# Retention queries projected feature-major, with a sine table kept in SBUF, in a hybrid decoder trunk

## The chip, the cores and the metric

The kernel runs on one core of one Trainium2 chip. The metric is the device time of one execution in microseconds; the time given for a kernel is the median of several executions. A core has five engines with instruction queues of their own: TensorE (PE in the profile; its weight loads are shown apart as PEld), VectorE (DVE), ScalarE (ACT), GpSimd (POOL) and SyncE (SP), which here only issues DMAs. PSUM has eight banks, into which TensorE writes.

## The reference

Two layers (`DEPTH`), sequence 1024, width 1024, batch 1, all in float32. Per layer:

```python
shift, scale, gate = jnp.split(c_act @ w_mod + b_mod, 3, axis=-1)
h = rms_norm(x, pre_gain) * (1.0 + scale) + shift
proj = h @ w_in        # columns: attention (q, k, v, gate), retention (q, k, v, gate), GLA
...
rq, rk = apply_rotary(rq, positions, ret_freq), apply_rotary(rk, positions, ret_freq)
r = retention(rq, rk, rv)
r_out = rms_norm(r) * silu(rg)
...
y = concat([a_out, r_out, g_out]) @ w_out
x = x + gate * rms_norm(y, post_gain)
```

`apply_rotary` splits a head's 64 features into halves x1, x2 and returns x1 cos - x2 sin and x2 cos + x1 sin, with an angle per position and frequency. Attention and retention have different frequencies, 32 each. `retention` has four heads of 64 features and works in chunks of 128 positions. Position i of a chunk has the decay g^(i+1) on its query and g^(-(i+1)) on its key (g is a constant of the head); the masked product of queries and keys is multiplied with the values, a 64x64 state per head carries what lies before the chunk, and after each chunk the state is multiplied by g^128. The result is RMS-normalised per position and head, with no gain.

## The kernel before

**Matmuls.** Every projection is a product of two float32 numbers split into a high and a low part (`F32R` tiles, index 0 and 1): three passes `(0,0), (1,0), (0,1)` over eight slices of the contraction, 24 matmuls per result (`accum`). `project` makes a token-major result: the normalised input `hT` of one tile of 128 positions is the loaded operand and 256 columns of a weight stream. `project_T` makes a feature-major result: 128 weight columns are loaded and 512 positions stream; the attention queries and gates use it. Weights arrive as 256 KB stages (`st`, from SyncE's queue), are split by ScalarE, VectorE and GpSimd, and lie in places of two arenas.

**Stages of a layer.** The gates of GLA and retention (gg, rg) by pairs of tiles; then retention, for each of four pairs `p` the projections rq, rk, rv of both tiles; then GLA, the attention keys and values, the attention queries and gates, and the output projection. In the first layer, before the gates, the first modulation is computed and x is normalised, modulated and transposed (`pre`, L657).

**Retention.** For rq and rk each, `ret_rot` (L1157) rotates a 128x256 result out of PSUM with five VectorE operations (`rotary`, L818) against `sincos`, the token-major table in SBUF, and multiplies it by the decay of the query (`qdec`) or the key (`kdec`, which holds the factor 1/8 too). rv is copied by ScalarE. `ret_core` (L1163) transposes q and k of a tile, two transposes each, copies all four blocks out of PSUM at once, multiplies scores, masks them by VectorE, and multiplies by v and by the state `stR`. `head_norm_gate` squares, reduces and normalises with `rstd_of` (L635), whose `eps` is an immediate.

**Tables.** `tables` (L414) computes all angles, 128 positions by 8 tiles by 64 frequencies, reduces them and takes sines and cosines: some fifteen VectorE operations of 512 elements in four `t2` tiles, with a pause between each two. `tables_T` (L447) then makes, for each pair, a copy of the attention half repeated for four heads, four transposes, a ScalarE copy with the factor 1/8, and a store to `tabS` in DRAM. `attn_rot` (L862) reads it back for the attention queries.

**Modulation.** The later modulations read `w_mod` in slices of 256 KB into tiles of their own (`mod_stage`, tag `sm8`, `BMOD` = 5 of them) and accumulate on VectorE (L367), a slice per step.

**Order.** TensorE's instructions run in the order in which the program writes them. A planner sets this order: `clk` adds the modelled time of each matmul, every other piece of work is a generator in `jobs` that yields a delay (a value of the table `L`, `key@1` for layer 1) or a flag, and `pump` runs whatever is due, after every seven matmuls. `await_flag` moves `clk` forward where something is not due. Thus the delays in `L` decide after how many matmuls a transpose or a small product is put into TensorE's stream; TensorE stands if its input is not there by then. The other engines' orders and SyncE's are set by the compiler's scheduler from the program's order and the dependences. `table_job` (L1460) starts with the layer; retention starts after `await_flag("tables")` (L1504).

**Buffers** that the change touches: `mm`, three PSUM banks for projections, and `aux`, five for all else; `kT0` and `kT1`, one buffer each, which hold two tiles of x at the start, the attention keys' high and low parts, and (kT1) the GLA gate input `gaT`; `mx`, two large tiles.

Of the kernel before, what the change touches and what calls it, by code (L numbers as in the profile page):

```python
# [60 lines left out]
def host_constants():  # L61
# [12 lines left out]
    c["qdec"] = (gam[None, :] ** (i[:, None] + 1.0)).astype(f)  # L74
    c["kdec"] = (0.125 * gam[None, :] ** (-(i[:, None] + 1.0))).astype(f)
# [18 lines left out]
def trunk(ctx: ExitStack, tc: tile.TileContext, ins, cst, out):  # L94
# [17 lines left out]

    def t2(dt=F32):
        return gp.tile([P, 512], dt, tag="t2", name=nm("t2"), bufs=B2)
# [6 lines left out]

    def mod_stage():
        return gp.tile([P, 512], F32, tag="sm8", name=nm("ms"), bufs=BMOD)
# [142 lines left out]
    tabS = dr.tile([NP_, P, 2, 256], F32, name="tabS")  # L266
# [147 lines left out]
    def tables():  # L414
        PIF = float(np.nextafter(np.float32(math.pi), np.float32(0)))
        ang = t2()
        V.tensor_tensor(ang.rearrange("p (t k) -> p t k", t=NT), posf.unsqueeze(2).to_broadcast((P, NT, 64)),
                        freq.unsqueeze(1).to_broadcast((P, NT, 64)), ALU.mult)
        yield
        nn = t2()  # L420
# [7 lines left out]
        n2 = t2()  # L428
# [4 lines left out]
        red = t2()  # L433
# [13 lines left out]
    def tables_T():  # L447

        for p in range(NP_):
            yield L["tt1"]  # L450
            rep_ = t2()
            V.tensor_copy(rep_.rearrange("p (s t h k) -> p s t h k", s=2, t=2, h=4),
                          sincos[:, 2 * p:2 * p + 2, :, 0:32].rearrange("p t s k -> p s t k").unsqueeze(3)
                          .to_broadcast((P, 2, 2, 4, 32)))
            yield L["tt2"]
            pt = aux()
            for i in range(4):
                transp(pt[:, i * P:(i + 1) * P], rep_[:, i * P:(i + 1) * P], ident)
            tb = t2()
            A.activation(tb, pt, AF.Copy, scale=0.125)  # L460
            nc.sync.dma_start(tabS[p], tb.rearrange("p (s n) -> p s n", s=2))
# [172 lines left out]

    def rstd_of(ss, w, scale, eps):  # L635
        r = small(w)
        V.tensor_scalar(r, ss, scale, eps, ALU.mult, ALU.add)  # L637
# [133 lines left out]
    qdec = cload("qdec")  # L771
    kdec = cload("kdec")
# [89 lines left out]
    def attn_rot(l, hf, g, w_):  # L862
# [3 lines left out]
        for s, d in ((0, sn), (1, cs)):  # L866
            nc.sync.dma_start(d.rearrange("p (s n) -> p s n", s=2),
                              tabS[2 * hf:2 * hf + 2, :, s, :].rearrange("s p n -> p s n"))
# [288 lines left out]
    def ret_rot(t, src, dec_):  # L1157
        r = t1()
        rotary(r, src, 4, t, 1)
        eng("rdec").tensor_tensor(h4(r), h4(r), dec_.unsqueeze(2).to_broadcast((P, 4, 64)), ALU.mult)  # L1160
# [564 lines left out]
```

## Time and profile before

| | |
|---|---|
| Median of 3 runs | 993.5 us (992.89 to 995.62) |
| Profiled execution | 992.12 us |
| its span, first to last instruction | 990.4 us |
| Mean granted TensorE clock | 0.991 |
| Instructions | 19626 |

The page gives for each engine its busy time, its share of the span and its instructions. A group line has: line, engine, operation, output<-inputs by tile names, shapes, count; then busy time and the mean of one in ns; then the idle time before it with what ended it. A wait line has: the waiting engine, tile and line, what it waited for, then microseconds in total, times, and the longest. A line of the timeline has: start, length, engine, line, what, count. A line of DMA issues has: what, queue, operation, count, KB each, median us from issue to landing.

### The profile page before, as it was taken

How to read it: one execution, taken by the hardware profiler on the slowest of the kernel's cores; microseconds unless marked ns; L12 is line 12 of the kernel's file. 1: busy time of each engine (PE TensorE's matmuls, PEld its weight loads, DVE VectorE, ACT ScalarE, POOL GpSimd, SP SyncE). 2: the span in 40 equal slices, each digit the busy share in tenths (PEclk: the TensorE clock that was granted, in tenths of full speed). 3: DMA queues.
4: the chain of work that ended last, by engine and by line, in shares of the span. 5: the costliest groups of instructions: out<-in, count | busy, mean ns of one | idle time of the engine just before them, and what ended most of it. 6: DMA issues, size and time to landing. Idle time of an engine off the chain costs nothing. (4 is left out here: it accounts for less than half of the span.)

```text
span 990.4 us, 19626 instructions
## 1 busy us (share of the span) xinstructions
PE 964.5 (97%) x7133; PEld 824.7 (83%) x7133; DVE 683.3 (69%) x1679; ACT 409.5 (41%) x1152; POOL 244.7 (25%) x310
## 2 busy tenths in 40 slices
PE   5899999999999999999999999999999999999996
PEld 1599999888998777778889999998999877777775
DVE  3879858687766777654787266775765577676975
ACT  2577312333332656623555242133332257664331
POOL 2322011233310224420124100122322034544000
PEclk8899999999999999999999999999999999999999
DMA  8853414532234355587565121342132433388783
GB/s 319 297 187 96 153 49 137 162 123 79 67 122 146 91 177 160 166 269 240 200 223 179 61 87 33 97 146 68 50 97 86 128 89 121 111 267 269 256 267 132
DMA packets 112305, 148.77 MB, mean 150 GB/s; under 512 B 12064, under 2 KB 63820, under 8 KB 112208
## 3 DMA queue, kind: packets, MB, share of 16 engines
q1 hardware_dynamic: 100176, 132.19, 42.4%
q10 hardware_dynamic: 12032, 15.33, 4.4%
q8 instruction: 56, 0.92, 0.4%
q14 instruction: 41, 0.34, 0.1%
HBM read 109.20 MB, written 36.18 MB: 147 GB/s over the span
## 5 line engine op out<-in xcount | busy, mean ns | idle before, releaser
L168 PE MATMUL mm<-arena 128*128 128x256 f32 (+2 forms) x1824 | 300.8, 319 | 1.7 <-ACT arena L707 1.5
L168 PE MATMUL mm<-arena,arena 128*128 128x256 f32 (+2 forms) x1824 | 296.0, 316 | 0.0
L168 PEld LDWEIGHTS mm<-arena 128*128 128x128 f32 x1824 | 255.3, 191 | 26.1 <-issue 3.6
L168 PEld LDWEIGHTS mm<-arena,arena 128*128 128x128 f32 x1824 | 251.6, 188 | 24.4 <-issue 4.0
L638 POOL TENSOR_TENSOR sm<-sm,mhalf 128x1 f32<-128x1 f32 (+1 forms) x64 | 55.7, 870 | 329.0 <-DVE sm L637 293.6
L168 PE MATMUL mm<-arena,mx 128*128 128x512 f32 (+1 forms) x564 | 130.9, 387 | 0.5 <-DMA mx<-mixS 0.3
L168 PEld LDWEIGHTS mm<-arena,mx 128*128 128x128 f32 x564 | 101.4, 188 | 24.7 <-issue 1.5
L152 ACT ACTIVATE t<-aux 128x256 f32<-128x256 f32 (+2 forms) x124 | 55.7, 466 | 65.1 <-PE aux L183 44.1
L152 ACT ACTIVATE arena<-st 128x512 fp32r<-128x512 f32 x94 | 56.1, 628 | 49.7 <-PE mm L168 21.2
L932 POOL TENSOR_TENSOR smx<-smx,sm 128x512 f32<-128x512 f32 x32 | 35.1, 1097 | 130.2 <-DVE sm L931 109.4
L536 DVE TENSOR_TENSOR arena<-st,arena 128x512 fp32r<-128x512 f32 x77 | 61.6, 821 | 2.9 <-ACT arena L152 1.6
L536 POOL TENSOR_TENSOR arena<-st,arena 128x512 fp32r<-128x512 f32 x31 | 44.3, 1431 | 75.5 <-ACT arena L152 68.0
L928 ACT ACTIVATE smx<-smx,sm 128x129 f32<-128x129 f32 x128 | 49.9, 392 | 29.9 <-DVE sm L925 29.9
L183 PE MATMUL aux<-c_ident,t 128*128 128x128 f32 (+1 forms) x292 | 47.9, 283 | 6.3 <-DVE t L669 5.7
L367 DVE SCALAR_TENSOR_TENSOR acc<-ms,c_act,acc 128x512 f32<-128x512 f32 x60 | 45.6, 759 | 5.3 <-DMA ms<-in_w_mod_dram 4.4
L183 PEld LDWEIGHTS aux<-c_ident,t 128*128 128x128 f32 (+1 forms) x292 | 35.4, 145 | 12.6 <-DVE t L669 7.3
L976 ACT ACTIVATE t<-aux 128x256 f32<-128x256 f32 x32 | 12.3, 384 | 76.6 <-PE aux L168 69.2
L168 PEld LDWEIGHTS aux<-t,mx 32*128 32x128 f32 (+1 forms) x896 | 40.0, 187 | 4.0 <-issue 2.4
L701 ACT ACTIVATE t<-aux,mod,mod 128x128 f32<-128x128 f32 x68 | 26.0, 460 | 39.4 <-PE aux L183 21.6
L168 PE MATMUL aux<-t,mx 32*128 32x32 f32 (+1 forms) x896 | 41.3, 272 | 0.2 <-DVE modg L381 0.2
L1251 DVE SCALAR_TENSOR_TENSOR t<-t,sm,t 128x512 f32<-128x512 f32 x32 | 24.0, 781 | 22.4 <-DMA t<-in_x_dram 16.7
L923 DVE COPY_PREDICATED smx<-c_curmask,aux 128x256 f32<-128x256 int32 x64 | 25.4, 446 | 16.6 <-ACT smx L152 13.2
(224 smaller groups left out, 1382.5 us busy)
## 6 DMA issues: line engine op xcount, KB each, us to landing
st<-in_w_in_dram SPq DMA_DIRECT2D x96, 256.0 KB, 4.1
ms<-in_w_mod_dram SPq DMA_DIRECT2D x64, 256.0 KB, 4.1
mx<-mixS SPq DMA_DIRECT2D x20, 512.0 KB, 5.4
st<-in_w_last_dram SPq DMA_DIRECT2D x36, 256.0 KB, 3.6
wm<-in_w_mod_dram SPq DMA_DIRECT2D x12, 512.0 KB, 6.6
t<-in_x_dram SPq DMA_DIRECT2D x24, 256.0 KB, 5.5
mixS<-t SPq DMA_DIRECT2D x40, 128.0 KB, 2.4
mixS<-t ACTq DMA_DIRECT2D x32, 128.0 KB, 1.9
```

Source lines behind the costliest of these rows:

```text
L152: A.activation(dst, src, AF.Copy)
L168: T.matmul(dst, lhsT, rhs, start=start, stop=stop)
L183: T.transpose(dst, src, idn)
L367: V.scalar_tensor_tensor(acc, wt, c_act[:, k:k + 1], acc, ALU.mult, ALU.add)
L536: e.tensor_tensor(lo, st, f(hi), ALU.subtract)
L638: G.tensor_tensor(r, r, mhalf[:, :w], ALU.pow)
L701: A.activation(hf[:, ks], at[kt], AF.Identity, scale=gain, bias=shift)
L923: V.copy_predicated(sv, curmask.unsqueeze(1).to_broadcast((P, 2, P)), pv[:, :, n // P - 1, :])
L928: A.activation(sm[:, h, :], sm[:, h, :], AF.Exp, bias=mx[:, h:h + 1], accum_out=sums[:, h:h + 1])
L932: eng("pn").tensor_tensor(sm[:, :, 0:128], sm[:, :, 0:128], rs.unsqueeze(2).to_broadcast((P, 4, P)), ALU.mult)
L976: A.activation(sq, po, AF.Square)
L1251: V.scalar_tensor_tensor(xt[j], yg[j], r, xt[j], ALU.mult, ALU.add)
```

## The change

- The queries of retention come from a new `ret_q`, once per pair of tiles and feature-major: `project_P` loads 128 weight columns and streams 256 positions, twice. The rotation's sine products are four VectorE operations on 32 partitions each, which write to the neighbouring block of 32 partitions, then one product with the cosines and one sum, all of 512 elements per partition. The table for it, `tab` (features by positions, sine and cosine, with the factor 1/8), stays in SBUF.
- The result lies in `kT0` (pairs 0 and 1) and `kT1` (pairs 2 and 3). `ret_core` no longer transposes q; it transposes k alone and waits for the flag of the queries, then takes its slice.
- Neither q nor k is multiplied by a decay. The key's decay is put on v (`vdec`), by VectorE in place of ScalarE's copy; the query's decay is a factor of a whole row, which the normalisation takes out, with a constant per row and head (`reps`) in place of `4 * EPS`.
- The tables are computed in one `mx` tile instead of four `t2` tiles, behind the last modulation so far. Two blocks of four transposes make both halves (attention and retention); they are stored to `tabS`, from which four DMAs of 256 KB fill `tab`; sixteen stores of 64 KB write the attention half to `tabA`, repeated for four heads. Retention waits for `tab` in the planner.
- `BMOD` goes from 5 to 3.
- Nearly all delays in `L` have other values, with new ones for `tt3`, `tt4`, `tt6` and `rq1`. Among them: `tb1` 24.5 to 12.59, `tb2` 0.75 to 0.89, `tt1` 8.6 to 7.12, `tt2` 5.32 to 1.62, `mod2` 4.0 to 3.86, `ld2` 0.21 to 1.2.

```diff
-    c["qdec"] = (gam[None, :] ** (i[:, None] + 1.0)).astype(f)
-    c["kdec"] = (0.125 * gam[None, :] ** (-(i[:, None] + 1.0))).astype(f)
+    c["reps"] = (4.0 * EPS * gam[None, :] ** (-2.0 * (i[:, None] + 1.0))).astype(f)
+    c["vdec"] = (gam[None, :] ** (-(i[:, None] + 1.0))).astype(f)
...
-    tabS = dr.tile([NP_, P, 2, 256], F32, name="tabS")
+    tabS = dr.tile([2, 2, 32, S], F32, name="tabS")
+    tabA = dr.tile([4, 32, 2, S], F32, name="tabA")
+    tab = cp.tile([P, 2, S], F32, name="tab")
...
-        ang = t2()
-        V.tensor_tensor(ang.rearrange("p (t k) -> p t k", t=NT), posf.unsqueeze(2).to_broadcast((P, NT, 64)),
-                        freq.unsqueeze(1).to_broadcast((P, NT, 64)), ALU.mult)
+        tmp = mix_tile(F32).rearrange("p a k q -> p (a k q)").rearrange("p (i n) -> p i n", i=4)
+        ang, nn, n2, red = (tmp[:, i] for i in range(4))
+        with tc.issue_after(mark[3].ins):
+            V.tensor_tensor(ang.rearrange("p (t k) -> p t k", t=NT), posf.unsqueeze(2).to_broadcast((P, NT, 64)),
+                            freq.unsqueeze(1).to_broadcast((P, NT, 64)), ALU.mult)
...
-        for p in range(NP_):
-            yield L["tt1"]
-            rep_ = t2()
-            V.tensor_copy(rep_.rearrange("p (s t h k) -> p s t h k", s=2, t=2, h=4),
-                          sincos[:, 2 * p:2 * p + 2, :, 0:32].rearrange("p t s k -> p s t k").unsqueeze(3)
-                          .to_broadcast((P, 2, 2, 4, 32)))
-            yield L["tt2"]
+        tbs = []
+        for i in range(2):
+            yield L["tt1"] if i == 0 else L["tt2"]
             pt = aux()
-            for i in range(4):
-                transp(pt[:, i * P:(i + 1) * P], rep_[:, i * P:(i + 1) * P], ident)
+            for t in range(4):
+                transp(pt[:, t * P:(t + 1) * P], sincos[:, 4 * i + t].rearrange("p s k -> p (s k)"), ident)
             tb = t2()
             A.activation(tb, pt, AF.Copy, scale=0.125)
-            nc.sync.dma_start(tabS[p], tb.rearrange("p (s n) -> p s n", s=2))
+            ts = slice(512 * i, 512 * i + 512)
+            nc.sync.dma_start(tabS[:, :, :, ts].rearrange("s c k n -> (s c k) n"), tb)
+            tbs.append(tb)
+        yield L["tt3"]
+        for b in range(4):
+            nc.sync.dma_start(tab[32 * b:32 * b + 32], tabS[:, 1].rearrange("s k n -> k s n"))
+        flag("tab", L["tt6"])
+        for i in range(2):
+            for h in range(4):
+                yield L["tt4"]
+                for j in range(2):
+                    nc.sync.dma_start(tabA[h, :, j, 512 * i:512 * i + 512], tbs[i][64 * j:64 * j + 32])
...
+    def project_P(pm, l, p, w, c):
+        h = hT[(l, p)]
+        accum(pm, lambda a, k: w[:, a, k, c:c + P], lambda b, k: h[:, b, k, 0:256])
...
-    def ret_rot(t, src, dec_):
+    def ret_q(l, p, w):
+        pm = mm()
+        for c in range(2):
+            project_P(pm[:, 256 * c:256 * c + 256], l, p, w, c * P)
...
+        sn, cs = (tab[:, i, 256 * p:256 * p + 256].unsqueeze(1).to_broadcast((P, 2, 256)) for i in range(2))
+        u, x = t2(), t2()
+        for b in range(4):
+            r = slice(32 * b, 32 * b + 32)
+            o = two(x)[32 * (b ^ 1):32 * (b ^ 1) + 32]
+            if b % 2:
+                V.scalar_tensor_tensor(o, two(pm)[r], -1.0, sn[r], ALU.mult, ALU.mult)
+            else:
+                V.tensor_tensor(o, two(pm)[r], sn[r], ALU.mult)
+        V.tensor_tensor(two(u), two(pm), cs, ALU.mult)
+        if p % 2 == 0:
+            rqT[0] = gp.tile([P, NT * P], F32, tag=f"kT{p // 2}", name=nm("rq"), bufs=1)
+        q = rqT[0][:, 512 * (p % 2):512 * (p % 2) + 512]
+        V.tensor_tensor(q, u, x, ALU.add)
+        flag(("rq", l, p), L["rq1"])
+        return two(q)
...
-            transp(pt[:, j * P:(j + 1) * P], q[:, j * P:(j + 1) * P], ident)
-            transp(pt[:, (2 + j) * P:(3 + j) * P], k[:, j * P:(j + 1) * P], ident)
-        tt_ = t2()
-        qT = tt_[:, 0:256]
-        kTt = tt_[:, 256:512]
-        copy("rT", tt_, pt)
+            transp(pt[:, j * P:(j + 1) * P], k[:, j * P:(j + 1) * P], ident)
+        kTt = t1()
+        with tc.high_priority():
+            copy("rT", kTt, pt[:, 0:256])
+        yield (0.0, ("rq", l, t // 2))
+        qT = q[:, :, P * (t % 2):P * (t % 2) + P]
...
-        await_flag("tables")
+        await_flag("tab")
         for p in range(NP_):
             last = p == NP_ - 1
-            rr = {}
-            for name in ("rq", "rk", "rv"):
+            q = ret_q(l, p, used(l, "rq"))
+            pump()
...
-                        copy("rv", v, src)
-                        job(ret_core(l, t, rr[("rq", tt)], rr[("rk", tt)], v))
+                        V.tensor_tensor(h4(v), h4(src), vdec.unsqueeze(2).to_broadcast((P, 4, 64)), ALU.mult)
+                        job(ret_core(l, t, q, ks[tt], v))
...
-B2, B1, BS, BST, MMB, SMB, BMOD = 10, 8, 11, 5, 3, 3, 5
+B2, B1, BS, BST, MMB, SMB, BMOD = 10, 8, 11, 5, 3, 3, 3
```

47 lines of the change are left out of this document (27 added, 20 removed).

## The prediction

> **What bounds the kernel now.** I read the page's busy shares first, then stretches of time, then TensorE's waits, then the timeline inside the retention stage.
>
> ```profile
> PE 964.5 (97%) x7133; PEld 824.7 (83%) x7133; DVE 683.3 (69%) x1679; ACT 409.5 (41%) x1152; POOL 244.7 (25%) x310
> ```
>
> Columns of the stretches: from:to, length, then busy time (and instructions) of PE, weight load, DVE, ACT, POOL, granted clock, DMA share, GB/s.
>
> ```profile
> 46.00:980.00 934.00, 930.58 (x7000) 806.19 (x6998) 652.21 (x1607) 390.80 (x1105) 230.57 (x287) 1.00 0.45 142
> ...
> 50.00:75.00 25.00, 25.00 (x211) 24.95 (x210) 19.99 (x55) 19.89 (x60) 6.79 (x15) 1.00 0.60 188
> 75.00:100.00 25.00, 24.84 (x206) 24.57 (x205) 24.82 (x55) 17.36 (x39) 5.77 (x10) 1.00 0.32 99
> 100.00:125.00 25.00, 25.00 (x218) 24.41 (x217) 20.84 (x64) 8.24 (x16) 1.86 (x1) 1.00 0.45 146
> ...
> 600.00:625.00 25.00, 25.00 (x217) 24.47 (x216) 15.43 (x52) 5.94 (x11) 2.02 (x2) 1.00 0.11 33
> ```
>
> From 46 to 980 us TensorE is idle for 934.00 - 930.58 = 3.4 us at the full clock. So the length of its own instruction stream sets the end: an instruction taken out of it is worth its whole pitch, and delays set better can win back at most 3.4 us there. The waits say the same:
>
> ```profile
> PE aux L183 <- DVE posr L408: 5.8, 1, 5.8
> PE aux L183 <- DVE t L669: 5.7, 3, 4.0
> PE mm L168 <- ACT arena L707: 1.5, 1, 1.5
> ```
>
> These three, 13.0 us, lie in the start or touch it, before layer 0's table work; nothing in the diff removes them.
>
> **Terms on TensorE.** The group that loses instructions, as the page has it, and the ends that its mean hides (matmuls are pipelined, so 283 ns is a latency):
>
> ```profile
> L183 PE MATMUL aux<-c_ident,t 128*128 128x128 f32 (+1 forms) x292 | 47.9, 283 | 6.3 <-DVE t L669 5.7
> ```
>
> In layer 1's retention stage, blocks of 2 and of 6 transposes, each with the instruction that follows:
>
> ```profile
> 606.66 0.38 PE L183 MATMUL aux<-c_ident,t 128*128 128x128 f32 x2
> 606.80 0.60 PE L168 MATMUL mm<-arena,arena 128*128 128x256 f32 x3
> ...
> 636.29 0.82 PE L183 MATMUL aux<-c_ident,t 128*128 128x128 f32 x6
> 636.86 3.08 PE L168 MATMUL mm<-arena,arena 128*128 128x256 f32 x24
> ```
>
> ```profile
> 101.73 0.60 PE L183 MATMUL aux<-c_ident,t 128*128 128x128 f32 x4
> 102.08 1.08 PE L168 MATMUL mm<-arena 128*128 128x256 f32 x7
> ```
>
> The next matmul starts 0.14, 0.57 and 0.35 us after the block's start, so a transpose more in a block costs (0.57 - 0.14)/4 = 0.107 us; the bare average of the shortest is 0.07. The change removes the two transposes of q in each `ret_core`: 2 x 8 tiles x 2 layers = 32, or 3.4 us. The tables need two blocks of four instead of four: -2 x 0.35 = -0.7 us. Together -4.1 us, with ends 40 x 0.07 = 2.8 and 40 x 0.107 = 4.3.
>
> The projection of q keeps its amount: 24 matmuls of 256 columns per tile before, 24 per half of the columns and pair of tiles after, so 48 per pair either way. What is loaded and what streams change places; both are 128x128 and 128x256. Nothing.
>
> Here is the one place where a page speaks against the sum. The Trainium skill, Perfetto Trace Analysis, section Identifying the Most-Contended Engine, calls matmul busy time a bad measure of headroom and wants LDWEIGHTS busy time. Over the whole kernel that is 83%, which would leave 17% of slack for removed work to vanish in. In the stage that changes the trace shows 24.47 of 25 us on weight loads, so by the rule, read stage by stage, the 4.1 us stand; by the whole-kernel figure the gain would be 0.83 x 4.1 = 3.4 us.
>
> **Terms on the other engines.**
>
> ```profile
> L826 DVE TENSOR_TENSOR t<-mm,sincos 128x256 f32<-128x256 f32 x32 | 13.3, 415 | 5.8 <-PE mm L168 5.8
> L831 DVE TENSOR_TENSOR t<-t,tr 128x128 f32<-128x128 f32 x32 | 10.1, 316 | 0.0
> L830 DVE TENSOR_TENSOR t<-t,tr 128x128 f32<-128x128 f32 x32 | 9.3, 291 | 0.0
> L828 DVE TENSOR_TENSOR tr<-mm,sincos 128x128 f32<-128x128 f32 x32 | 9.0, 280 | 0.0
> L829 DVE TENSOR_TENSOR tr<-mm,sincos 128x128 f32<-128x128 f32 x32 | 8.9, 279 | 0.0
> L1160 DVE TENSOR_TENSOR t<-t,c_qdec 128x256 f32<-128x256 f32 x16 | 6.7, 417 | 0.2
> ...
> L873 DVE TENSOR_TENSOR t<-mm,t 128x512 f32<-128x512 f32 x16 | 11.0, 689 | 18.5 <-PE mm L168 18.3
> L981 DVE TENSOR_TENSOR t<-aux,sm 128x256 f32<-128x256 f32 x32 | 13.6, 425 | 28.9 <-POOL sm L638 28.9
> L1201 DVE TENSOR_TENSOR stR<-stR,aux 64x128 f32<-64x128 f32 x28 | 7.9, 282 | 1.3 <-PE aux L168 1.0
> L452 DVE COPY t<-sincos 128x512 f32<-128x512 f32 x4 | 1.7, 416 | 0.0
> ```
>
> VectorE, per pair of tiles. Before: four rotations of 0.415 + 0.280 + 0.279 + 0.291 + 0.316 = 1.58 us and four decay multiplies of 0.417: 8.0 us. After: two rotations of k, 3.2; two multiplies of v by its decay out of PSUM, 2 x 0.425 (L981 has the same shape and source) = 0.85; and q's six operations of 512 elements. Four of these work on 32 partitions, a shape the trace lacks: by the partition count they would cost a quarter of L873, 0.17, by the free length all of it, 0.689. I take 0.689, because 64 partitions of 128 elements (L1201, 282 ns) cost what 128 partitions do (L828, 280). So q is 6 x 0.689 = 4.1, the pair 8.1, eight pairs +1.0 us in all; the four copies of L452 go, -1.7. Where retention runs, VectorE has 4.2 us (layer 0, 100 to 125) and 9.6 us (layer 1, 600 to 625) idle in 25: hidden. If that cover were gone, the +0.1 us of each pair would show, 1 us. The per-row constant `reps` replaces an immediate in an operation of 4 elements: nothing.
>
> ```profile
> L152 ACT ACTIVATE t<-aux 128x512 f32<-128x512 f32 x48 | 28.5, 593 | 26.7 <-PE aux L183 20.0 <-DVE t L1605 4.2 <-ACT t L152 0.8
> L152 ACT ACTIVATE t<-aux 128x256 f32<-128x256 f32 x44 | 16.8, 382 | 16.3 <-PE aux L168 9.1 <-PE aux L183 5.5 <-DVE tr L829 1.4
> L152 ACT ACTIVATE t<-mm 128x256 f32<-128x256 f32 x40 | 15.1, 380 | 42.4 <-PE mm L168 36.4 <-ACT t L152 3.3 <-DMA mixF<-t 1.6
> ```
>
> ScalarE loses 16 x (0.593 - 0.382) + 16 x 0.380 = 9.5 us, and is 41% busy: worth nothing by itself. But v's PSUM bank is now freed by VectorE, and q holds one of the three `mm` banks for five reads, 5 x 0.689 = 3.4 us, where a tile of q held it for 0.97.
>
> **The table's new path.**
>
> ```profile
> L452 DVE COPY t<-sincos x4: 411/416/421, 93.5 to 144.8; 128x512 f32<-128x512 f32 x4
> ```
>
> ```profile
> L461 SPq DMA_DIRECT2D tabS<-t x4: 320/326/384, 106.2 to 152.4; - x4
> ```
>
> ```profile
> ms<-in_w_mod_dram SPq DMA_DIRECT2D x64, 256.0 KB, 4.1
> ...
> wm<-in_w_mod_dram SPq DMA_DIRECT2D x12, 512.0 KB, 6.6
> ...
> t<-tabS SPq DMA_DIRECT2D x16, 256.0 KB, 4.0
> ...
> tabS<-t SPq DMA_DIRECT2D x4, 256.0 KB, 2.0
> ```
>
> Before, the planner's due times put the end of the sines at 24.5 + 15 x 0.75 = 35.8 us after the layer's start and the first table transpose at 35.8 + 8.6 + 5.3 = 49.7; the trace has them at 93.5 and 101.7, offsets of 57.7 and 52.0. After, the plan is 12.59 + 15 x 0.89 = 25.9 for the sines, 33.1 and 34.7 for the transposes. With the same offsets the sines end near 83.6 and TensorE reaches the transposes at 85.1 and 86.7: a margin of 1.5 us where it was 8. I cost the margin at nothing, since some of the table work now runs between 50 and 75, where VectorE has 5.0 us idle, not between 75 and 100, where it has 0.2.
>
> From 86.7: block 0.35, copy 0.59, issue 0.33, landing 2.0, four issues of 0.33, landing. Four reads of 256 KB take 4.0 at least (they overlap) and 16 at most (one behind the other); nearest is the 512 KB row, 6.6, which I take. `tab` lands at 95.3, 97.9 or 107.3. It is needed when q of the first pair is done, about 101.7 (TensorE's instruction after it starts at 102.08). TensorE then has two tiles of k, 48 x 0.122 = 5.8 us (0.122 from the 24 matmuls' 3.08 less a tail of about 0.15), before v needs q's bank: it stalls only if `tab` is later than 101.7 + 5.8 - 3.4 = 104.1. So 0, with 3.2 us at the far end.
>
> SyncE's queue gets 22 table DMAs for 4: 18 x 0.33 = 5.9 us of issue, the 16 stores of the attention table two at a time between weight loads. Behind its waits (for ScalarE's copy, and 2.0 us for the store to land) stand the loads of rk and rv; rk has the whole of q, 5.8 us, as cover. Zero, at most the 2.0 of that wait.
>
> Three tiles for the modulation: a tile makes a round in 0.75 + 0.33 + 4.1 = 5.2 us, three are wanted every 3 x 3.86 = 11.6. Zero, as long as SyncE is not held for more than 6.4 us.
>
> **Sum.** The profiled execution took 992.1 us, its span 990.4 and 1.7 around it: 992.1 - 4.1 = 988.0. It lies 1.4 below the median of 993.5; against the median the sum is 989.4, which I predict. A difference of 0.3%, 3.0 us, is about what a measurement of this kernel can tell from no change.
>
> **Rivals.**
>
> First, short new waits eat the gain: the margin of 1.5 us at the transposes, 2.0 in SyncE's queue, 3.2 at `tab`. For it: VectorE's 24.82 of 25 us before the stage, and bank and queue margins that all shrink together. Against it: only layer 0 can be hit. Two of the three, some 3 us, give 992.4.
>
> Second, slower: the sines are not ready earlier. Place: TensorE at the first table transpose, near 85.1. If VectorE, full from 75 to 100, ends them at 93.5 as before, TensorE, which takes its instructions in order, stands for 8.4 us. The trace shows what a stop costs besides:
>
> ```profile
> 17.50:20.00 2.50, 1.97 (x8) 1.57 (x8) 2.36 (x7) 0.00 (x0) 0.78 (x1) 0.50 1.04 392
> 20.00:22.50 2.50, 1.65 (x8) 1.57 (x8) 1.54 (x3) 1.89 (x3) 1.47 (x3) 0.50 1.05 342
> ```
>
> ```profile
> 18.00 1.97 PE L183 MATMUL aux<-c_ident,t 128*128 128x128 f32 x8 [3.98 <-DVE t L669]
> ```
>
> After the 4.0 us wait for L669 (it ends at 18.0) the clock is 0.50 for 5 us, which loses 2.5. Price 8.4 + 2.5, so 989.4 + 10.9 = 1000.3; it makes the kernel slower from 7.1 us on, that is, from sines later than 89.7. Against it: they start 12 us earlier in the plan. The Trainium skill, TensorE: Matmul & The Clock Gate, section Why this matters for your kernels, warns of idle gaps over about 3 us, after which the clock falls to half; by that rule, the trace agrees (0.50 after 4.0 us).
>
> Third, better: the new delays also win back 2.5 of the 3.4 us idle between 46 and 980, giving 986.9, at the most 986.0. Against it: each remaining wait is 0.8 us or less.
>
> Fourth, the transposes were no bound, and nothing is won: 993.5. Against it stands the packed stream.
>
> **How the numbers follow.** Forecast 0.50 (own range 988.0 to 990.4, from the bounds of the transposes and a wait or two of some tenths); first rival 0.20; second 0.13, half of it between 996.5 and 1000; third 0.10; fourth 0.05; the rest, 0.02, slower for a cause not named. Faster by over 0.3% means below 990.5: 0.60. Within: 0.25. Slower: 0.15. The range of 985.5 to 997.0 leaves out most of the second rival and little else.
>
> **What would show it.** Group L183 with the identity and `t` should have 40 instructions fewer (292 to 252); retention blocks should show 2 transposes; TensorE's idle time between 46 and 980 should stay near 3.4 us; q's four 32-partition operations near 689 ns; no row of the waits should name `tab`, `sincos` or the table's copy with more than 1 us; VectorE should show no new wait for the modulation's tiles. Wrong would be: a wait of TensorE between 80 and 110 of several us, a second stretch at clock 0.50, or blocks of transposes that take as long as before.

## The result and the profile after

The changed kernel takes 991.03 us (median of 22 runs, 988.21 to 996.32); the kernel before, run beside it, 995.09 (22 runs, 992.84 to 999.73). The ratio is 0.9967, 95% interval 0.9956 to 0.9979: 3.3 us faster, between 2.1 and 4.4. The forecast was 4.1 us. The profiled execution of the change has a span of 988.1 us, 2.3 shorter than the one of before.

The page's busy shares after the change, then the stretch that was read for the kernel before (from:to, length, then busy time and instructions of PE, weight load, DVE, ACT, POOL, granted clock, DMA share, GB/s):

```profile
PE 962.2 (97%) x7093; PEld 820.9 (83%) x7093; DVE 692.2 (70%) x1627; ACT 399.5 (40%) x1135; POOL 244.6 (25%) x310
```

```profile
46.00:980.00 934.00, 929.37 (x6981) 804.75 (x6980) 663.93 (x1559) 381.48 (x1091) 232.65 (x289) 1.00 0.46 144
```

TensorE is still the bound: 40 instructions fewer (7133 to 7093), and idle for 934.00 - 929.37 = 4.6 us in this stretch where it was 3.4. But a fixed stretch of time does not hold the same work in both kernels; over the whole span TensorE is idle for 25.9 us in both (990.4 - 964.5, 988.1 - 962.2). The same work lies between the starts of two projections that both kernels have: the first of layer 0, and one of layer 1's output that reads the tile `ma`. Between them the two traces have the same matmuls but for the 40 transposes. First the kernel before, then the change:

```profile
37.21 1.05 PE L168 MATMUL mm<-arena 128*128 128x272 f32 x4
922.39 5.76 PE L168 MATMUL mm<-arena,ma 128*128 128x512 f32 x24
```

```profile
37.45 0.77 PE L168 MATMUL mm<-arena 128*128 128x272 f32 x4
921.89 5.76 PE L168 MATMUL mm<-arena,ma 128*128 128x512 f32 x24
```

The last three columns are runs of the experiments below:

| us | before | change | change, profiled again | before, new delays | before, three tiles |
|---|---|---|---|---|---|
| from the first start to the second | 885.18 | 884.44 | 884.80 | 888.47 | 886.38 |
| from the second to the end of the span | 68.0 | 66.2 | 68.6 | 70.2 | 70.1 |

So when that projection starts, TensorE has gained 0.4 to 0.7 us on the kernel before, not 4.1: 3.4 to 3.7 us have gone to new costs. On the old structure with the new delays it has gained 3.7 to 4.0, and on the one with three tiles, which the change has too, 1.6 to 1.9. Most of the 3.3 us that the runs show must then lie behind 922 us, or in executions unlike the profiled ones. Of it, 0.7 us lie behind the start of TensorE's last projection (979.01 to 990.4 is 11.4 us, 977.43 to 988.1 is 10.7). The stretch in front of it, from 922 us on, differs by 2.4 us between two profiles of the same kernel, and the profiled execution of before (992.12 us) is faster than all 22 that were measured beside the change, so what the change gains there is not shown.

The identity transposes, from the page's groups and from the answer on the identity's tile:

```profile
L183 PE MATMUL aux<-c_ident,t 128*128 128x128 f32 (+1 forms) x244 | 41.8, 283 | 6.4 <-DVE t L684 4.6 <-ACT t L1122 0.8 <-DVE mx L1138 0.7
```

```profile
L183 PE MATMUL aux<-c_ident,sincos x8: 271/272/273, 85.1 to 87.9; 128*128 128x128 f32 x8
```

244 + 8 = 252, as many as were to remain of 292. Where the idle time lies is read by stages; first the kernel before, then the change, the stages in which they differ by more than 0.2 us:

```profile
46.00:66.00 20.00, 19.15 (x160) 18.89 (x158) 16.17 (x42) 13.20 (x37) 8.02 (x15) 1.00 0.50 146
66.00:100.00 34.00, 33.84 (x281) 33.54 (x280) 32.13 (x76) 26.14 (x64) 7.19 (x12) 1.00 0.45 140
100.00:133.00 33.00, 33.00 (x286) 32.41 (x285) 26.32 (x83) 8.62 (x17) 4.00 (x3) 1.00 0.35 114
...
560.00:720.00 160.00, 159.79 (x1432) 150.42 (x1431) 108.60 (x310) 51.47 (x125) 31.20 (x39) 1.00 0.26 81
...
900.00:980.00 80.00, 79.51 (x349) 63.18 (x348) 60.92 (x105) 24.93 (x54) 12.40 (x12) 1.00 0.75 240
```

```profile
46.00:66.00 20.00, 19.86 (x165) 19.59 (x164) 18.29 (x47) 13.29 (x39) 7.28 (x14) 1.00 0.45 135
66.00:100.00 34.00, 32.92 (x269) 32.15 (x268) 30.42 (x69) 26.81 (x63) 9.28 (x13) 1.00 0.48 142
100.00:133.00 33.00, 32.29 (x271) 31.09 (x270) 25.14 (x55) 7.60 (x15) 2.41 (x2) 1.00 0.53 167
...
560.00:720.00 160.00, 158.96 (x1425) 149.61 (x1425) 112.55 (x287) 46.84 (x117) 32.12 (x40) 1.00 0.28 86
...
900.00:980.00 80.00, 80.00 (x364) 64.31 (x364) 62.08 (x107) 25.93 (x58) 11.51 (x13) 1.00 0.72 237
```

Idle time of TensorE (length less PE's busy time), before and after:

| stretch, us | what runs | before | after |
|---|---|---|---|
| 46 to 66 | end of the start, layer 0 | 0.85 | 0.14 |
| 66 to 100 | gates, and now the tables | 0.16 | 1.08 |
| 100 to 133 | retention, layer 0 | 0.00 | 0.71 |
| 560 to 720 | retention and GLA, layer 1 | 0.21 | 1.04 |
| 900 to 980 | end of the output | 0.49 | 0.00 |

The first row is a shift only: from its first projection to the next group TensorE takes 13.0 us in both kernels (37.21 to 50.24, 37.45 to 50.49). The three stretches that lost are the ones that the change touches. TensorE's timeline there (start, length, engine, line, what, count; in brackets the idle time before it and what ended it):

```profile
75.11 1.66 PE L168 MATMUL mm<-arena,arena 128*128 128x272 f32 x10 [0.59 <-ACT arena L722]
...
82.48 2.75 PE L168 MATMUL mm<-arena 128*128 128x256 f32 x21 [0.49 <-DVE t L1009]
85.07 0.60 PE L183 MATMUL aux<-c_ident,sincos 128*128 128x128 f32 x4
...
87.62 0.60 PE L183 MATMUL aux<-c_ident,sincos 128*128 128x128 f32 x4
...
110.97 0.51 PE L168 MATMUL mm<-arena,arena 128*128 128x256 f32 x2 [0.33 <-ACT arena L152]
111.77 4.42 PE L168 MATMUL mm<-arena,arena 128*128 128x256 f32 x32 [0.29 <-ACT arena L152]
```

```profile
655.26 2.73 PE L168 MATMUL mm<-arena,arena 128*128 128x256 f32 x21 [1.04 <-DVE t L1188]
```

Two waits in the gates (1.08), two for weights that ScalarE splits (0.62), one for the PSUM bank that q's rotation still reads (1.04; L1188 is the product with the cosines, its last reader). None is at the table's transposes, which run at 85.07 and 87.62 without a wait, and none names `tab`. The rows of the table's path:

```profile
L446 DVE TENSOR_SCALAR sincos<-sincos x1: 601/601/601, 82.3 to 82.3; 128x512 f32<-128x512 f32 x1
```

```profile
L1187 DVE TENSOR_TENSOR t<-mm,tab x16: 680/686/691, 104.5 to 653.0; 32x512 f32<-32x512 f32 x16
...
L463 SPq DMA_DIRECT2D tab<-tabS x4: 319/425/429, 94.7 to 96.0; - x4
```

The sines end at 82.9 (82.3 + 0.60), the transposes come 2.2 us later, the table is asked for from 94.7 on, and q's first operation starts at 104.5, when TensorE has made q.

One number is far from the forecast: VectorE is busy 692.2 us where it was 683.3, 8.9 us more; the terms were +1.0 and -1.7. The instructions have the lengths that were taken. What was wrong is that lengths were added up. VectorE's timeline in the last pair of layer 1:

```profile
650.30 0.68 DVE L1187 TENSOR_TENSOR t<-mm,tab 32x512 f32<-32x512 f32 x1
...
653.01 0.69 DVE L1187 TENSOR_TENSOR t<-mm,tab 32x512 f32<-32x512 f32 x1
653.71 0.69 DVE L1185 SCALAR_TENSOR_TENSOR t<-mm,tab 32x512 f32<-32x512 f32 x1
654.42 0.69 DVE L1188 TENSOR_TENSOR t<-mm,tab 128x512 f32<-128x512 f32 x1
655.03 0.42 DVE L983 TENSOR_TENSOR t<-aux,t 128x256 fp32r<-128x256 f32 x1
...
658.18 0.41 DVE L841 TENSOR_TENSOR t<-mm,sincos 128x256 f32<-128x256 f32 x1
658.51 0.27 DVE L843 TENSOR_TENSOR tr<-mm,sincos 128x128 f32<-128x128 f32 x1
...
659.31 0.68 DVE L544 TENSOR_TENSOR arena<-st,arena 128x512 fp32r<-128x512 f32 x1
```

A token-major rotation takes 659.31 - 658.18 = 1.13 us of the engine, not the 1.58 that its five lengths add up to: each instruction starts about 0.08 before the one ahead of it is done. The operations on 32 partitions do not gain that: 0.70 from one start to the next. By starts, a pair cost 4 x 1.13 + 4 x 0.33 = 5.8 us before (0.33 for a decay, the step of the 256-column operation at 658.18) and costs 2 x 1.13 + 2 x 0.33 + 4 x 0.70 + 2 x 0.61 = 6.9 now; eight pairs make +8.8, less 1.3 for the four copies of the old tables: +7.5 of the 8.9.

### The profile page after: what moved, and what is told of

Same layout as the page of the kernel before. It is cut to its first block, busy times and chain, and to the rows that moved or that the text cites. A ratio compares the mean times of both kernels' runs of the same rounds, so it can differ in the third digit from the quotient of the medians.

```text
span 988.1 us, 19451 instructions
## 1 busy us (share of the span) xinstructions
PE 962.2 (97%) x7093; PEld 820.9 (83%) x7093; DVE 692.2 (70%) x1627; ACT 399.5 (40%) x1135; POOL 244.6 (25%) x310
## 4 chain that ended last, share of the span: by engine, by line
PE 84%; DVE 7%; DMA 5%; issue 1%; POOL 1%; ACT 1%; POOLq 0%; DVEq 0%; SPq 0%; ACTq 0%
PE mm L168 64%; PE aux L168 16%; PE aux L183 4%; DMA wm<-in_w_mod_dram 3%; POOL sm L653 1%; DVE arena L544 1%; DMA st<-in_w_in_dram 1%; DMA ms<-in_w_mod_dram 1%; DMA t<-in_x_dram 1%; DVE t L1292 0%; DVE t L684 0%; DVE arena L726 0%; DVE t L1185 0%; DVE t L1187 0%; DVE t L1076 0%
## 5 line engine op out<-in xcount | busy, mean ns | idle before, releaser
L653 POOL TENSOR_TENSOR sm<-sm,mhalf 128x1 f32<-128x1 f32 (+1 forms) x64 | 58.9, 921 | 314.0 <-DVE sm L650 174.5
L152 ACT ACTIVATE t<-aux 128x256 f32<-128x256 f32 (+2 forms) x124 | 52.4, 437 | 94.8 <-PE aux L183 79.4
L544 POOL TENSOR_TENSOR arena<-st,arena 128x512 fp32r<-128x512 f32 x31 | 43.2, 1395 | 83.0 <-ACT arena L152 77.4
L544 DVE TENSOR_TENSOR arena<-st,arena 128x512 fp32r<-128x512 f32 x77 | 61.3, 813 | 2.7 <-ACT arena L152 1.5
L369 DVE SCALAR_TENSOR_TENSOR acc<-ms,c_act,acc 128x512 f32<-128x512 f32 x60 | 45.4, 756 | 18.0 <-DMA ms<-in_w_mod_dram 17.4
L183 PE MATMUL aux<-c_ident,t 128*128 128x128 f32 (+1 forms) x244 | 41.8, 283 | 6.4 <-DVE t L684 4.6
L183 PEld LDWEIGHTS aux<-c_ident,t 128*128 128x128 f32 (+1 forms) x244 | 29.5, 144 | 14.0 <-DVE t L684 6.6
```

The costliest lines, as they stand in the source:

```text
L152: A.activation(dst, src, AF.Copy)
L183: T.transpose(dst, src, idn)
L369: V.scalar_tensor_tensor(acc, wt, c_act[:, k:k + 1], acc, ALU.mult, ALU.add)
L544: e.tensor_tensor(lo, st, f(hi), ALU.subtract)
L653: G.tensor_tensor(r, r, mhalf[:, :w], ALU.pow)
```

## The experiments

Each ratio is to the kernel before, measured beside it; 0.001 is 1.0 us. The change itself was measured in two such sets of runs and gave 0.9967 and 0.9944, so between two sets a difference of less than about 2 us says nothing. Where a set can't tell, the stretch of the table above is given, from layer 0's first projection to the one on `ma`: it is 884.44 and 884.80 us in the two profiles of the change. Unless said otherwise the edit is to the changed kernel.

### What a transpose costs

Two more transposes of k in each block of `ret_core`, into a part of the bank that nobody reads (32 in all); then six more (96). The planner's clock does not count them.

```diff
             transp(pt[:, j * P:(j + 1) * P], k[:, j * P:(j + 1) * P], ident)
+            T.transpose(pt[:, (2 + j) * P:(3 + j) * P], k[:, j * P:(j + 1) * P], ident)
```

> The changed kernel, with two more transposes of k in every block of the retention core, whose results nobody reads: 32 instructions of the kind that the change removed, at the same places, with the order of everything else untouched. Theory (the gain is TensorE's pitch, 0.107 us a transpose, on a packed stream): 3.4 us slower than the changed kernel, so about 0.7 us below the kernel before plus what the new waits cost, near ratio 0.9995 to 1.001. Rival (removed transposes were covered by other waits): no slower than the changed kernel, ratio 0.9967.

> As the run with two, but six more transposes in every block, 96 in all: the same price three times over, to have it clear of noise. Theory: 96 x 0.107 = 10.3 us slower than the changed kernel, ratio to before about 1.007. Rival (cover): under 5 us slower, ratio below 1.002.

Measured: 994.97 us, ratio 1.0001 (0.9987 to 1.0015); and 1000.56, ratio 1.0046 (1.0029 to 1.0062). Against the change's 0.9967 that is 3.4 us for 32, or 0.107 each, and 7.9 for 96, or 0.082 each, less than the 10.3 expected; against its second measurement, 0.9944, it is 5.7 and 10.2. The traces are closer together: the stretch takes 888.67 and 894.11 us, 3.9 to 4.2 us more for 32 (waits beside the longer blocks included) and 9.3 to 9.7 for 96, 0.10 each. The first one's timeline, blocks of four where the change has two:

```profile
588.62 0.27 PE L183 MATMUL aux<-c_ident,t 128*128 128x128 f32 x1
...
588.94 0.27 PE L1208 MATMUL aux<-c_ident,t 128*128 128x128 f32 x1
```

Three steps take 588.94 - 588.62 = 0.32. So the term of the sum stands, with an uncertainty of a microsecond: 32 transposes are worth some 3 to 4 us, and the rival by which they were no bound falls.

### The new structure, the new delays, and one without the other

The change with every delay of before (the new keys and `tt1`, `tt2` as in the change):

> The changed kernel with the delays of before for every key that both have (the keys of the table's new path stay as in the change, tb1 and tb2 go back to 24.5 and 0.75). Theory (the gain is TensorE's work, the new delays give or take at most the 3.4 us of waits that the kernel before had): faster than the changed kernel or slower by up to 3 us; but the table starts 12 us later, so that retention of layer 0 waits for it, some 5 us more: ratio to before 0.998 to 1.004. Rival (the delays bring the gain): above 1.004.

Measured: 1010.06, ratio 1.0128 (1.0098 to 1.0158), 16 us slower than the change, far outside the theory's range; it lies in the rival's, which the next run rules out. Its stretch and the longest wait of TensorE in it behind the start:

```profile
46.00:980.00 934.00, 916.07 (x6871) 792.66 (x6869) 648.84 (x1533) 375.61 (x1077) 231.83 (x287) 0.99 0.44 141
```

```profile
PE mm L168 <- ACT kept L1385: 3.2, 1, 3.2
```

TensorE is idle for 17.9 us, 13 more than in the change, in pieces of up to 3.2 us over both layers, and the granted clock falls too (0.50 from 705 to 710 us). The late tables are a part of it; set back alone, below, they cost 10 us. But they are made in layer 0 only, and from layer 1's first gates to the first projection behind GLA this run takes 198.3 us (531.02 to 729.33), the change 190.0 (522.55 to 712.57): 8 us that are not theirs. The delays say after how many matmuls each small product comes; that the old ones put products ahead of their inputs, now that q is finished elsewhere and later, is argued from waits such as these, not tested one by one.

The kernel before with the new delays (all keys that both have, except `tt1`, `tt2`):

> The kernel before with the delays of the change for every key that both have, tt1 and tt2 left as before. Theory (delays alone give at most a few tenths of the waits): within 2 us of the kernel before, ratio 0.998 to 1.003. Rival (the delays bring the gain): 0.9967 or less. If the new delays cost something by themselves, which the later retention start of the changed kernel suggests, above 1.001.

Measured: 996.64, ratio 1.0022 (1.0003 to 1.0041): the new delays alone make the old structure some 2 us slower (0.3 to 4.1). Its timeline has the same two waits in the gates as the change, at the old kernel's lines:

```profile
76.79 1.66 PE L168 MATMUL mm<-arena,arena 128*128 128x272 f32 x10 [0.96 <-ACT arena L707]
...
84.19 3.11 PE L168 MATMUL mm<-arena 128*128 128x256 f32 x24 [0.55 <-DVE t L995]
```

So these two come with the new delays, not with q; that it is the early tables among them is borne out below, where the tables come 3.9 us later and both waits are gone. The gain is the new structure's, but only with delays fitted to it; the two can't be added as separate parts. The change also gives priority to ScalarE's copy of the transposed k and to VectorE's masks of the scores; no run takes that away alone.

### When the tables are made

The tables' first delay alone set back to that of before:

```diff
-"tb1": 12.59
+"tb1": 24.5
```

> The changed kernel with one delay put back: the table work starts 24.5 us after the layer in the planner, not 12.59. Theory (the earlier table work on VectorE is what slows the gates of layer 0 by 2.3 us in the trace, and only the early start lets the table land in time): the 384 gate matmuls of layer 0 take about 2 us less than in the changed kernel, and retention starts later or stands, because the table lands some 10 us later than at 100; together 2 to 6 us slower than the changed kernel, ratio to before 0.999 to 1.003. Rival (the early start costs nothing, the gates are slow for another reason, such as the other delays): gates as slow as in the changed kernel, and the whole 5 us or more slower, above 1.002.

Measured: 1002.22, ratio 1.0071 (1.0047 to 1.0094), 10 us more than the change, in the rival's range. TensorE's timeline, and the granted clock (the third number from the right) of stretches after it:

```profile
97.27 0.29 PE L183 MATMUL aux<-c_ident,ga 128*48 128x128 f32 x1 [0.40 <-POOL ga L1018]
98.81 7.42 PE L168 MATMUL mm<-arena,arena 128*128 128x256 f32 x48 [1.24 <-DVE t L1009]
```

```profile
97.50:100.00 2.50, 1.26 (x7) 1.20 (x7) 2.33 (x3) 1.76 (x6) 1.34 (x1) 0.81 0.54 122
100.00:102.50 2.50, 2.50 (x14) 2.50 (x13) 2.50 (x12) 0.19 (x2) 0.00 (x0) 0.50 0.73 243
```

The 48 matmuls take 7.42 us, where 48 x 0.122 = 5.9 is usual. The gates do not come sooner, as the theory had it: their waits become longer, and the clock halves after them. The table is late as well: it is asked for at 110.5 instead of 94.7, TensorE stands 2.4 us at 122 for q's sum (L1192), and the clock halves again (0.59 from 122.5 to 125), as it does a third time after a wait of 1.9 us for ScalarE (L1122) at 221.5.

The other side: the margin at the table's transposes taken away.

```diff
-"tt1": 7.12
+"tt1": 3.0
```

> One delay of the changed kernel is lowered: the first table transposes are due 4.1 us sooner (tt1 7.12 to 3.0), the sines are not. In the profile of the change the sines ended at 82.9 us and the transposes began at 85.1, so they would now come up at about 81.0, 1.9 us ahead of the sines. Theory (the margin decides: TensorE takes its instructions in order): a wait of TensorE at the first transpose of 1 to 2 us, no stretch at half clock, since the wait is well below the 4 us that was followed by one, and 1 to 2 us more than the change: ratio to the kernel before 0.9975 to 0.9990. Rival (the margin is worth nothing, VectorE or the order of the work gives way): the ratio of the change, 0.9967, within 0.001.

Measured: 993.54, ratio 0.9979 (0.9963 to 0.9995); the change beside it 989.97. TensorE's timeline and clock:

```profile
82.23 1.05 PE L183 MATMUL aux<-c_ident,sincos 128*128 128x128 f32 x4 [3.03 <-DVE sincos L446]
82.94 3.51 PE L168 MATMUL mm<-arena 128*128 128x256 f32 x17
86.28 0.60 PE L183 MATMUL aux<-c_ident,sincos 128*128 128x128 f32 x4
```

```profile
82.50:85.00 2.50, 2.50 (x13) 2.50 (x12) 1.57 (x5) 2.49 (x7) 0.27 (x1) 0.50 0.29 98
85.00:87.50 2.50, 2.50 (x20) 2.50 (x20) 1.62 (x4) 1.01 (x4) 0.00 (x0) 0.86 0.47 157
```

This is the mechanism of the second rival, at the place it was given: TensorE stands 3.0 us for the sines, and then runs at half clock, against what was expected. The block of four and the 17 matmuls after it take 86.28 - 82.23 = 4.05 us instead of 0.35 + 17 x 0.122 = 2.4, so the clock loses 1.6 us more. Of these 4.7 us the runs show 3.6 (993.54 - 989.97): when everything comes later, the change's wait of 0.49 for L1009 is gone, and the 38 matmuls that begin near 110 take 5.2 us (113.29 to 118.48) instead of 6.0 (110.02 to 116.03), since their weights come less late. So the margin of 2 us decides: it costs nothing while it holds, and its loss costs more than its size.

### SyncE's queue

The sixteen stores of the attention table were let out more slowly.

```diff
-"tt4": 1.15
+"tt4": 6.0
```

> The changed kernel with the sixteen stores of the attention table 6.0 us apart by twos instead of 1.15, so that they no longer stand in SyncE's queue between the loads of rk and rv. Theory (the stores delay these loads, and TensorE pays 0.6 us of visible waits for ScalarE's weight split at 111 us, about 1 us with the ends that the records hide): 0.5 to 1.5 us faster than the changed kernel, ratio to before 0.995 to 0.9965. Rival (the loads are late because their stages are freed late): no difference, 0.9967.

> The change itself, beside the next kernel on the same chip, so that the two can be compared directly. Both theories: ratio 0.9956 to 0.9979 to the kernel before.

> The changed kernel with the stores of the attention table spread (tt4 1.15 to 6.0) once more, beside the change itself. Theory (SyncE's queue held the loads of rk and rv behind these stores, which cost the change about 1.5 us in layer 0): 1 to 2 us below the change in the same call. Rival (the 1.9 us between two calls was chance): the same time as the change within 0.5 us.

Measured: 989.59, ratio 0.9948 (0.9933 to 0.9963); in a second set of runs 989.42, ratio 0.9936 (0.9917 to 0.9955), beside the change's 989.97, ratio 0.9944 (0.9925 to 0.9963). SyncE's queue in the change, and in the first run with the stores spread:

```profile
102.11 1.86 SPq L469 DMA_DIRECT2D tabA<-t  x4
104.01 0.43 SPq L157 DMA_DIRECT2D st<-in_w_in_dram  x1
```

```profile
101.94 1.40 SPq L157 DMA_DIRECT2D st<-in_w_in_dram  x3
```

The weight stages went out ahead of the stores. In the second run with them spread, the stretch of retention that holds the two waits for weights in the change is in one piece:

```profile
109.63 4.66 PE L168 MATMUL mm<-arena,arena 128*128 128x256 f32 x38
```

The same 38 matmuls take 6.0 us in both profiles of the change, from 110.02 to 116.03 in the first, and 4.5 here, 109.63 to 114.12. So the queue did hold up weights, for 1.5 us at its place, of which only 0.62 shows as idle time. It stays gained up to the projection on `ma`: the stretch takes 883.24 and 883.17 us in the two profiles with the stores spread, 1.2 to 1.6 less than in the two of the change. What it is worth in the end is not settled: 0.5 us within one set of runs, where 1 to 2 were expected and the intervals overlap, and 1.9 across two. The end of the kernel does not hold still: the second profile of the change has waits there that the first has not (0.00 idle in the first):

```profile
900.00:980.00 80.00, 78.62 (x344) 61.57 (x341) 61.64 (x104) 25.89 (x57) 12.36 (x13) 1.00 0.75 245
```

The spread stores are faster than the kernel before in both sets, and in neither slower than the change.

Spread stores with the tables 3.9 us later (`tt4` 6.0 and `tb1` 16.5):

> The changed kernel with the stores of the attention table spread (tt4 1.15 to 6.0, as before) and the table work 3.9 us later (tb1 12.59 to 16.5). Theory (the waits of 0.59 and 0.49 us in the gates stage come from VectorE and ScalarE carrying the table work between 65 and 83 us): with the work moved 3.9 us these two waits go or move, sines end near 86.8, the table is issued near 98.6 and lands near 103, still ahead of its first use at 104.5; 0.5 to 1 us faster than the stores spread alone: ratio near 0.994. Rival (there is no slack left at the late side: q of the first pair waits for the table, as with tables 12 us later): 1 to 3 us slower than the stores spread alone, ratio 0.996 to 0.998, with a wait at q's additions or at the bank behind it.

Measured: 996.65, ratio 1.0005 (0.9989 to 1.0022), 7.2 us more than the spread stores alone beside it. Neither theory named the place. The table was in time, no wait names it, and the two waits of 75 and 82 are gone. In their stead:

```profile
101.36 5.44 PE L168 MATMUL mm<-arena,arena 128*128 128x256 f32 x31 [3.12 <-DVE t L1009]
```

```profile
102.50:105.00 2.50, 2.50 (x13) 2.50 (x13) 2.40 (x8) 1.04 (x3) 0.00 (x0) 0.50 0.97 229
```

L1009 is the last operation of a gate's silu, which frees the gate's bank. On VectorE eight of the modulation's slices (L369) and a splitting of weights of 1.79 us (L544) ran between 88 and 100 us, and the one that TensorE wanted started behind them at 100.91; then the clock halved. At 118 TensorE waits once more, 1.40 and 0.30 us for weights that VectorE splits (L544), and the clock halves a second time (0.50 from 120 to 122.5). That the later tables pushed those slices there is argued from the order, not shown by a run of its own. Shown is how narrow the place is: 4 us earlier at the transposes cost 3.6 us and 4 us later at the sines 7.2, where the whole change gains 3.3.

### q's bank, and the modulation's tiles

q's six VectorE operations given priority over other VectorE work:

```diff
         u, x = t2(), t2()
+        with tc.high_priority():
...
```

> The changed kernel with the six VectorE operations of the queries' rotation put ahead of other work that is ready. Theory (q holds a PSUM bank for 3.4 us and TensorE pays 1.0 us for it once, at 132 us): that wait goes, up to 1 us faster than the changed kernel, ratio to before 0.9955 to 0.9967. Rival (the bank's wait only moves to k or to the sums of GLA's decays, which now run later): no difference or slower by up to 1 us.

Measured: 993.47, ratio 0.9987 (0.9971 to 1.0004), about 2 us more than the change and more than either theory allowed; the trace bears it out (887.15 us in the stretch). The wait for L1188 is gone from the profile; in its place stand waits of 1.6 us for the operation that `head_norm_gate` ends with (L996), 0.8 for a rotation of k (L846) in the same stretch, and others of 1.0 to 1.4 elsewhere. The clock halves after the first two (0.68 from 660 to 662.5, 0.64 to 665). This way the bank's wait is moved, not removed: VectorE carries it all in one order.

The kernel before with three tiles for the modulation:

```diff
-B2, B1, BS, BST, MMB, SMB, BMOD = 10, 8, 11, 5, 3, 3, 5
+B2, B1, BS, BST, MMB, SMB, BMOD = 10, 8, 11, 5, 3, 3, 3
```

> The kernel before with three tiles of its own for the modulation's slices instead of five, all else untouched. Theory (a round of a tile takes 5.2 us and three are wanted every 11.6): no difference, ratio 0.999 to 1.001, VectorE's wait for the tiles' DMAs goes from 4.4 us to some 17 as in the changed kernel, and TensorE does not see it. Rival (SyncE is held longer than the 6.4 us that three tiles bear, VectorE stands, TensorE with it): slower by 1 to 3 us, 1.001 to 1.003.

Measured: 996.17, ratio 1.0011 (0.9996 to 1.0027): no difference that can be told. VectorE's wait for the slices does grow, from 4.4 us in the profile of before:

```profile
DVE acc L367 <- DMA ms<-in_w_mod_dram: 14.4, 12, 3.0
```

No wait of TensorE names these sums, so the 10 us stay beside its work. Up to the projection on `ma` its trace is 1.2 us longer than that of before (886.38 against 885.18); whether the tiles cost that is not shown.

## Why the prediction was right, and where it was not

**What bounds the kernel: right.** TensorE's stream sets the end, and what leaves it is worth its pitch. The first experiment gives the 32 transposes 3.4 us by the runs, the figure of the sum, and about 4 by the trace. The 0.7 us of the two table blocks was not measured by itself; the two that remain take 0.35 us each, as the trace of before had it.

**Projection of q, ScalarE: right.** ScalarE lost 10.0 us (409.5 to 399.5; 9.5 forecast), which bought nothing.

**The 32-partition operation: right in length** (0.686 against 0.689 taken, not 0.17). **VectorE's sum: wrong.** The step that added up the lengths (8.0 us a pair before, 8.1 after, +1.0 in all) took overlapping instructions at full length; by their starts a pair went from 5.8 to 6.9, and VectorE's busy time rose by 8.9 us instead of falling by 0.7. The cover was wide enough for most of it, but not free: q's five reads of its bank were put at 3.4 us and took 4.8 in the last pair (650.30 to 655.11), with other work between them, and TensorE stood 1.04 us for that bank. The statement that only layer 0 can be hit was wrong with it.

**The margin at the transposes: right by its outcome.** The sines were forecast at 83.6 and came at 82.9, the transposes at 85.1 and 86.7 and came at 85.07 and 87.62. But the price named for a loss, 2.5 us for the clock, was too high: it was read from 5 us at half clock in the start, where that lasted some 6.8, and the run without the margin lost 1.6. The statement behind it, that work between 50 and 75 lies in VectorE's slack there, was wrong in part: the chain of the tables ran to 83, and the gates waited 0.59 and 0.49, with the new delays in the old structure too.

**The table's path: right in that it costs nothing.** It was asked for at 94.7 instead of some 90, since its second store went out at 90.4 instead of 87.6 and took 4.2 us to land, not 2.0, but q was later too, at 104.5 instead of 101.7.

**SyncE's queue, costed at zero, at most 2.0: 1.5 us at its place,** 0.62 of it idle. The cover named for it, the 5.8 us of q, did not hold: the weights stood behind stores, and with the stores spread the stop is gone.

**Three tiles, costed at zero: right**, and the wait that was to be absent, VectorE's for the slices, is there (17.4 us in the change's waits, 4.4 before) and hidden.

**The step that failed** is the one that put all else at nothing and let TensorE's idle time "stay near 3.4 us". By the starts of the same projections TensorE was 0.4 to 0.7 us ahead when the projection on `ma` began, so that 3.4 to 3.7 of the 4.1 us were used up. The rows name some 3.8: the gates' waits (1.08, 0.16 before), SyncE's queue (1.5), q's bank (1.04 of idle time in its stretch, 0.21 before), and 0.55 between the first projection behind GLA in layer 1 and the one on `ma` (922.39 - 713.62 = 208.77 before, 921.89 - 712.57 = 209.32 after). This last comes with the new delays: the old structure with them has 209.32 too, the new one with the old delays 208.77. It is the first rival's mechanism, short new waits, at its full price of some 3 us.

**The number is in good part luck.** The runs gained 3.3 us all the same, with an interval from 2.1 to 4.4 that holds the forecast. But no term of the sum lies behind 922 us, where by the profiles most of the gain must be, and its cause there stays open; only the 0.7 us behind the start of TensorE's last projection can be placed.

Of the other rivals, the second is a real danger that the chosen delays avoid by 2 us; the third, a gain from the delays themselves, has the old structure with the new delays against it; the fourth falls with the transposes put back.

## What to carry to other kernels

Where TensorE's stream is packed, an instruction taken out of it is worth its pitch, but the small products around it were placed for the old lengths: count on some tenths to 1.5 us of new cost at each place that the change makes later, and fit the delays before judging it (with the old ones this change was 13 us slower than no change). Compare the starts of the same instruction in both traces: idle time in a fixed stretch showed 1.2 us of new waits here, where the starts showed over 3. Price work on VectorE by the distance between starts in the timeline, not by lengths, and look at how long it holds a PSUM bank with other work in between. Give an early input a margin on the safe side: 2 us of it cost nothing here, and losing it cost TensorE its wait and half as much again in clock.

## What the runs showed of the hardware

**The clock falls after short stops, here mostly for the same time.** It was halved after single waits of 3.03 and 3.12 us, and after shorter ones that followed each other: 0.40 and 1.24 us within 1.6 us (the run with the tables 12 us later), 1.60 and 0.76 (q first on VectorE), 1.40 and 0.30 (the tables 3.9 us later). The waits of 0.59 and 1.04 us in the change had no such effect: the 21 matmuls after the second took the usual 0.12 us each. Nor had one of 2.40 us at 119.8 in the run with the old delays, where the granted clock stayed at 1.00 up to 127.5, while one of 2.38 in the run with the tables 12 us later had it. So the length of a single wait does not decide, and the runs do not show what else does. Worked out from the granted clock of the stretches, these halvings lasted some 3.4 us each (with the margin taken away, all of 82.5 to 85, at 0.86 another 0.28 x 2.5 = 0.7 us, and some 0.2 before 82.5), which loses 1.7; in the start of the kernel before it was twice as long (0.90, 0.50, 0.50 and 0.73 in the four stretches of 2.5 us from 15 on). The Trainium skill, TensorE: Matmul & The Clock Gate, section Part 1: The HAM clock gate, gives a window of about 3.4 us for this; the trace agrees on the length. On the gap that it takes, over about 3 us in the section that the prediction named, the trace agrees for the two long waits and differs for the shorter ones, such as 1.24 us after 0.40.

**VectorE does a 32x512 operation no faster than a 128x512 one** (0.686 against 0.692 us), and holds the engine longer: 0.70 us from start to start, where the 128x512 one at 654.42 is followed after 0.61. The Trainium skill, VectorE: DVE Perf Modes, section Two Vector instructions with no wait between them, says that an instruction whose input or output begins in another group of 32 partitions than the last one's starts only when all earlier ones are done. The trace agrees: q's four operations change that group each time, and alone of the rows shown do not overlap.
